# A decoder layer on one core: first transfers swapped, a root in three steps, and a last residual shared with GpSimd

## The chip, the cores and the metric

The kernel runs on one core of a Trainium2 chip. A core has five engines that run their own instruction streams and wait for one another through semaphores: TensorE (PE; its weight loads are shown as PEld), VectorE (DVE), ScalarE (ACT), GpSimd (POOL) and SyncE (SP), which here only starts transfers. Matmul results go to PSUM; everything else lies in SBUF; inputs, weights and the result lie in the chip's main memory (HBM) and come and go by DMA. The metric is the time of one execution on the device in microseconds (us), as the median of several runs.

## The reference

One decoder layer for 512 tokens of width 1024, in float32. With `rms(x, g)` for the normalisation by the root of the mean square:

```python
f = swiglu(rms_norm(h, ffn1_norm_pre[l]), ffn1_w_gate[l], ffn1_w_up[l], ffn1_w_down[l])   # width 2816
h = h + 0.5 * rms_norm(f, ffn1_norm_post[l])
u = rms_norm(h, mix_norm_pre[l])
proj = u @ w_in[l]                       # q, k, v, recurrence inputs, gates
...                                      # dilated attention and a gated linear recurrence
merged = gates[:, :, 0] * attn_d + gates[:, :, 1] * rec_d
h = h + rms_norm(merged @ w_out[l], mix_norm_post[l])
f = swiglu(rms_norm(h, ffn2_norm_pre[l]), ffn2_w_gate[l], ffn2_w_up[l], ffn2_w_down[l])
h = h + 0.5 * rms_norm(f, ffn2_norm_post[l])
```

So there are three sub-layers (feed-forward, mixer, feed-forward), each with a normalisation ahead of it and one behind it, and a residual sum.

## The kernel before

The layer is computed transposed: the 1024 channels lie on 8 chunks of 128 partitions, the 512 tokens along the free dimension. The residual stream `h` is eight chunks of 128 x 512 in two tiles of four; `hm(m, sl)` is chunk m, `hpair(m, sl)` chunks m and m + 1. Where the order matters the tokens are cut into two halves of 256 (`HALVES`).

Each float32 product is made of three matmuls (`mm3`, `seven`): weights and activations are split into a rounded high part (ScalarE copies it, L255) and the remainder (VectorE subtracts, L256), by `split`; `hi*hi`, `hi*lo` and `lo*hi` are summed in PSUM. In the feed-forwards, all but the first five of 22 inner blocks go through a scheme with seven half-size products in place of eight (`seven`, its operands made by `w_forms` and `x_forms`).

Weights are one long stream in the order of their use. SyncE's queue transfers it in groups of up to 1 MB into two buffers (`raw`, L203); a buffer is refilled when VectorE has read the group before the last. `fetch_start` does the same for the very first weights, in eight pieces of 128 x 512, interleaved with the eight token chunks: token chunk k (L238), then weight piece k (L242), with the table of gains and biases `sm` (L240) behind the first token chunk.

The start: for k = 0 to 7, `pre_norm` scales token chunk k by its gain and splits it (L342 ScalarE, L343 VectorE; the gain is in `sm`), `split` splits weight piece k, `sq_add` squares the chunk for the norm (ScalarE L314 and L317, VectorE adds, L320), and twelve matmuls follow. The root of the norm is applied behind the matmuls, since it is one factor for each token.

The root, `rstd`: a matmul with ones sums the squares over the channels (L325, L327), ScalarE takes an approximate reciprocal root `y` (L329), and VectorE refines it by one Newton step in four instructions (L330 to L333), on 256 tokens at a time. There are six such roots, twelve halves: one for each normalisation.

The end of each sub-layer, `last_product`: the last matrix product's eight chunks are added up, squared and scaled by the output gain; when the first half's sum is there, its root follows, and `residual` multiplies two chunks by the root (L357) and adds them to `h` (L358), both on VectorE. At the end of the kernel both halves take all eight chunks in this way; `to_out` sends each chunk half out on SyncE's queue as soon as it is added (L1072), 128 KB each, sixteen in all. GpSimd's queue only moves the residual stream out and in again (L673, L677, L907, L1069, L1080).

The order in which an engine's instructions stand is set by a scheduler, which takes the program text, priorities (`tc.high_priority`) and its own estimates of durations; the instruction streams are then fixed, and each engine and each queue works its stream in order, waiting where it has to. Tiles of one tag share a fixed number of buffers (`bufs`): PSUM has five of tag `acc` and three of tag `aux`, each 128 x 512.

Of the kernel before, what the change touches and what calls it, by code (L numbers as in the profile page):

```python
# [148 lines left out]
def hybrid_layer(ctx: ExitStack, tc: tile.TileContext, xT: bass.AP, wst: bass.AP, small: bass.AP,  # L149
# [23 lines left out]
    def hm(m, sl=slice(0, T)):  # L173

        return hs["t"][m // 4][:, m % 4, sl]
# [4 lines left out]
    def col(name, i):  # L180
        o, w = SMALL[name]
        return sm[:, o + i:o + i + 1]
# [50 lines left out]
    def fetch_start():  # L233

        raws = [wpool.tile([P, RAW_W], F32, name="raw", tag="raw", bufs=2) for _ in range(2)]
        wts = []
        for k in range(KC):
            nc.sync.dma_start(hm(k), xT[k])  # L238
            if k == 0:
                nc.sync.dma_start(sm, small)  # L240
            raw = raws[k // 4][:, (k % 4) * 512:(k % 4) * 512 + 512]
            nc.sync.dma_start(raw, bass.AP(tensor=wst.tensor, offset=wst.offset + k * 512 * P,  # L242
                                           ap=[[512, P], [1, 512]]))
            if k % 2 == 0:
                wt = w8()
            o = (k % 2) * 512
            wts.append((wt[:, 0, o:o + 512], wt[:, 1, o:o + 512], raw))
        state["g"], state["off"] = KC, KC * 512 * P
        return wts
# [57 lines left out]
    def ntile(name, bufs):  # L307
        return tpool.tile([P, HB], F32, name=name, tag="c", bufs=CB)
# [13 lines left out]
    def rstd(acc, r, sl, extra=None):  # L322
        for s in halves(sl):
            ps = aux_ps()[:, :HB]
            PE.matmul(ps, ones, acc[:, s], start=True, stop=extra is None)  # L325
            if extra is not None:
                PE.matmul(ps, ones, extra, start=False, stop=True)  # L327
            v, y = ntile("v", 2), ntile("y", 2)
            ACT.activation(y, ps, AF.Abs_reciprocal_sqrt, bias=eps, scale=1.0 / D)  # L329
            DVE.tensor_scalar(v, ps, 1.0 / D, EPS, op0=ALU.mult, op1=ALU.add)  # L330
            DVE.tensor_mul(v, v, y)
            DVE.scalar_tensor_tensor(v, v, -0.5, y, op0=ALU.mult, op1=ALU.mult)
            DVE.scalar_tensor_tensor(r[:, s], v, 1.5, y, op0=ALU.add, op1=ALU.mult)  # L333

    def warm(acc):
# [3 lines left out]
    def pre_norm(x, gname, m, sl):  # L339

        z = hm(m, sl)
        ACT.activation(x.hi[m][:, sl], z, AF.Copy, scale=col(gname, m))  # L342
        DVE.scalar_tensor_tensor(x.lo[m][:, sl], z, col(gname, m), x.hi[m][:, sl].bitcast(F32),  # L343
                                 op0=ALU.mult, op1=ALU.subtract)
# [5 lines left out]

    def gain(gi, m):
        return ghalf[:, gi * 8 + m:gi * 8 + m + 1] if gi is not None else col("gmb", m)

    def residual(rp, m, sl):

# [4 lines left out]
    def last_product(key, x, evac, gi, nxt, then, slots, end=False):  # L360
# [24 lines left out]
                    rstd(acc, rp, HALVES[0], tails[0])  # L385
        for sl in HALVES:
            if sl.start:
                rstd(acc, rp, sl, tails[HB])
            for m in range(KC):
                if m % 2 == 0:  # L390
                    residual(rp, m, sl)
                nxt(sl, m)
        if then:
# [250 lines left out]
    r1 = npool.tile([P, T], F32, name="r", tag="r", bufs=2)  # L644
    for k in range(KC):
        wh, wl, raw = wts[k]
        pre_norm(u1, "g1a", k, FULL)
        split(wh, wl, raw)
        sq_add(acc, lambda s: hm(k, s), FULL, k == 0)
        if k == KC - 1:  # L650
            rstd(acc, r1, FULL)
        for j in range(4):
            js = slice(j * P, (j + 1) * P)
            mm3(first[j], wh[:, js], wl[:, js], u1.hi[k], u1.lo[k], k == 0, k == KC - 1)
# [414 lines left out]
        nc.gpsimd.dma_start(kept[i], hs["t"][i].rearrange("p k t -> p (k t)"))  # L1069

    def to_out(sl, m):
        nc.sync.dma_start(out[m][:, sl], hm(m, sl))  # L1072

    def wide():
        return big([P, 2, 1024])
# [110 lines left out]
```

## Time and profile before

| | us |
|---|---|
| median of 3 runs | 1261.55 |
| lowest and highest of them | 1261.41, 1261.65 |
| the profiled execution | 1260.8 |
| its span (first to last instruction) | 1259.0 |
| TensorE busy | 1238.1 |
| VectorE busy | 970.9 |
| ScalarE busy | 705.0 |
| GpSimd busy | 20.0 |

The granted clock of TensorE is 0.997 of full speed over the span. In the rows of the timeline the columns are start, duration, engine, line, operation, output, inputs, shape and count; a bracket gives the idle time of the engine before the instruction and what ended it. Lines are those of this kernel. A matmul row's duration is longer than the step to the next one, since matmuls are pipelined: gaps are read from the brackets. "SPq" is SyncE starting a transfer. Two rows with the same start to start distance are more telling than their durations, which overlap by some hundredths where instructions of one engine follow one another.

### The profile page before, as it was taken

Reading aid. Unit: us, or ns where it says so; the run is one execution under the profiler, and the core shown is the slowest. Engines: PE = TensorE matmul, PEld = TensorE weight load, DVE = VectorE, ACT = ScalarE, POOL = GpSimd, SP = SyncE. Lnnn points to the kernel's source line nnn. Section 1 sums busy time; section 2 is a strip of 40 time slices with the busy share of each in tenths; the row PEclk is TensorE's granted clock in tenths of the full one; section 3 lists DMA queues with packets and bytes.
Section 4 is the critical chain, followed back from the end, with each engine's and each line's share of the span. In section 5 each row is a group of like instructions: output and inputs, shape, how many; then the busy total and the mean of one; then the engine's idle time right before and its main releaser. Section 6 shows DMA issues by size and latency. Waiting matters only on the chain.

```text
span 1259.0 us, 19558 instructions
## 1 busy us (share of the span) xinstructions
PE 1238.1 (98%) x7952; PEld 1127.9 (90%) x7952; DVE 970.9 (77%) x1561; ACT 705.0 (56%) x1183; POOL 20.0 (2%) x42
## 2 busy tenths in 40 slices
PE   9999999999999999999999999999999999999996
PEld 7889999999888999999988888889988999999995
DVE  7987777786588788889676987753998777777755
ACT  6555444454555565566736879436555544445543
POOL 0000000001002000000100000000000000000000
PEclk9999999999999999999999999999999999999998
DMA  6122332233514232221342231322222222223332
GB/s 240 67 92 98 106 107 106 106 108 133 202 67 157 103 107 79 74 104 68 135 144 91 87 115 67 134 99 103 101 101 92 93 100 101 101 101 117 105 130 67
DMA packets 26937, 135.66 MB, mean 108 GB/s; under 512 B 3424, under 2 KB 5600, under 8 KB 14688
## 3 DMA queue, kind: packets, MB, share of 16 engines
q1 hardware_dynamic: 24192, 122.88, 27.8%
q0 software_dynamic: 2656, 11.54, 2.7%
q8 instruction: 62, 1.02, 0.3%
q14 instruction: 27, 0.22, 0.1%
HBM read 127.07 MB, written 6.29 MB: 106 GB/s over the span
## 4 chain that ended last, share of the span: by engine, by line
PE 79%; DVE 13%; ACT 4%; DMA 2%; issue 2%; SPq 0%; DVEq 0%; ACTq 0%
PE acc L270 11%; PE acc L269 11%; PE acc L268 11%; PE acc L512 10%; PE acc L513 10%; PE acc L514 10%; DVE w L256 3%; PE aux L514 2%; PE aux L513 2%; PE aux L512 2%; DMA raw<-in_w 2%; PE acc L719 1%; ACT w L255 1%; PE acc L721 1%; PE acc L720 1%
## 5 line engine op out<-in xcount | busy, mean ns | idle before, releaser
L256 DVE TENSOR_TENSOR w<-raw,w 128x1024 fp32r<-128x1024 f32 (+2 forms) x307 | 301.7, 988 | 107.0 <-ACT w L255 106.8
L255 ACT ACTIVATE w<-raw 128x1024 fp32r<-128x1024 f32 (+2 forms) x307 | 262.3, 867 | 189.0 <-PE aux L514 55.1
L512 PE MATMUL acc<-big,w 128*128 128x256 f32 x928 | 263.4, 284 | 0.2 <-ACT c L519 0.2
L513 PE MATMUL acc<-big,w 128*128 128x256 f32 x928 | 263.4, 284 | 0.0
L514 PE MATMUL acc<-big,w 128*128 128x256 f32 x928 | 263.1, 284 | 0.0
L268 PE MATMUL acc<-act,w 128*128 128x512 f32 (+1 forms) x524 | 192.0, 367 | 2.4 <-ACT w L255 2.3
L269 PE MATMUL acc<-act,w 128*128 128x512 f32 (+1 forms) x524 | 191.5, 366 | 1.2 <-DVE act L256 1.2
L270 PE MATMUL acc<-act,w 128*128 128x512 f32 (+1 forms) x524 | 190.5, 365 | 1.6 <-DVE w L256 1.6
L512 PEld LDWEIGHTS acc<-big,w 128*128 128x128 f32 x928 | 177.8, 192 | 2.2 <-ACT c L519 0.8
L513 PEld LDWEIGHTS acc<-big,w 128*128 128x128 f32 x928 | 177.8, 192 | 1.4
L514 PEld LDWEIGHTS acc<-big,w 128*128 128x128 f32 x928 | 177.9, 192 | 0.0
L519 ACT ACTIVATE c<-acc 128x256 f32<-128x256 f32 x166 | 63.3, 382 | 97.9 <-PE acc L514 92.1
L270 PEld LDWEIGHTS acc<-act,w 128*128 128x128 f32 x524 | 98.9, 189 | 18.5 <-DVE w L256 2.9
L268 PEld LDWEIGHTS acc<-act,w 128*128 128x128 f32 x524 | 98.8, 189 | 18.5 <-ACT w L255 3.9
L269 PEld LDWEIGHTS acc<-act,w 128*128 128x128 f32 x524 | 99.0, 189 | 16.1 <-DVE act L256 1.8
L268 PE MATMUL acc<-big,w 128*128 128x512 f32 (+1 forms) x240 | 91.7, 382 | 0.0
L270 PE MATMUL acc<-big,w 128*128 128x512 f32 (+1 forms) x240 | 91.7, 382 | 0.0
L269 PE MATMUL acc<-big,w 128*128 128x512 f32 (+1 forms) x240 | 91.7, 382 | 0.0
L513 PE MATMUL aux<-big,w 128*128 128x256 f32 x272 | 77.0, 283 | 0.0
L514 PE MATMUL aux<-big,w 128*128 128x256 f32 x272 | 77.0, 283 | 0.0
L512 PE MATMUL aux<-big,w 128*128 128x256 f32 x272 | 76.9, 283 | 0.0
L256 DVE TENSOR_TENSOR w<-s,w 128x1024 fp32r<-128x1024 f32 x50 | 61.0, 1221 | 5.0 <-ACT w L255 4.9
(273 smaller groups left out, 2412.9 us busy)
## 6 DMA issues: line engine op xcount, KB each, us to landing
raw<-in_w SPq DMA_DIRECT2D x89, 1024.0 KB, 4.8
raw<-in_w SPq DMA_DIRECT2D x23, 512.0 KB, 3.6
raw<-in_w SPq DMA_DIRECT2D x6, 768.0 KB, 4.3
raw<-in_w SPq DMA_DIRECT2D x16, 256.0 KB, 3.6
raw<-in_w SPq DMA_DIRECT2D x3, 896.0 KB, 4.6
h<-in_x SPq DMA_DIRECT2D x8, 256.0 KB, 5.4
h<-in_x POOLq DMA_DIRECT2D x8, 256.0 KB, 5.2
kept_m<-h POOLq DMA_DIRECT2D x2, 1024.0 KB, 4.5
```

The source lines that it names most:

```text
L255: ACT.activation(dh, src, AF.Copy)
L256: DVE.tensor_sub(dl, src, dh.bitcast(F32))
L268: PE.matmul(ps, wh, xh, start=first, stop=False)
L269: PE.matmul(ps, wh, xl, start=False, stop=False)
L270: PE.matmul(ps, wl, xh, start=False, stop=last)
L512: PE.matmul(ps, wh, xh, start=start and k == 0, stop=False, skip_group_check=True)
L513: PE.matmul(ps, wh, xl, start=False, stop=False, skip_group_check=True)
L514: PE.matmul(ps, wl, xh, start=False, stop=k == 3, skip_group_check=True)
L519: ACT.activation(c, ps, AF.Copy)
L719: PE.matmul(pss[b], um.hi[k][:, bl], wh[:, i, :], start=k == 0, stop=False)
L720: PE.matmul(pss[b], um.hi[k][:, bl], wl[:, i, :], start=False, stop=False)
L721: PE.matmul(pss[b], um.lo[k][:, bl], wh[:, i, :], start=False, stop=k == KC - 1)
```

## The change

There are four edits.

1. In `fetch_start` the weight piece k is transferred ahead of the token chunk k, and in the loop that uses them `split` of the weights stands ahead of `pre_norm` of the tokens. The table `sm` is now third on the queue, behind the first weight piece and the first token chunk.
2. In `rstd` the step from the mean square to the root takes three VectorE instructions in place of four: `(ps + D*EPS) * y`, then times `-0.5/D * y`, then `(v + 1.5) * y`. All twelve half-roots use it.
3. For the last half of tokens at the end of the kernel a new function, `residual_end`, takes the place of four calls of `residual`. The root `rp` of that half is written to PSUM. ScalarE copies it to SBUF (`rq`); GpSimd multiplies and adds chunks 6 and 7; VectorE does chunks 0 to 5 in pairs, with its products in PSUM.
4. `to_out` sends two chunks in one transfer of 256 KB, eight transfers in place of sixteen.

```diff
         for k in range(KC):
+            raw = raws[k // 4][:, (k % 4) * 512:(k % 4) * 512 + 512]
+            nc.sync.dma_start(raw, bass.AP(tensor=wst.tensor, offset=wst.offset + k * 512 * P,
+                                           ap=[[512, P], [1, 512]]))
             nc.sync.dma_start(hm(k), xT[k])
             if k == 0:
                 nc.sync.dma_start(sm, small)
-            raw = raws[k // 4][:, (k % 4) * 512:(k % 4) * 512 + 512]
-            nc.sync.dma_start(raw, bass.AP(tensor=wst.tensor, offset=wst.offset + k * 512 * P,
-                                           ap=[[512, P], [1, 512]]))
...
             ACT.activation(y, ps, AF.Abs_reciprocal_sqrt, bias=eps, scale=1.0 / D)
-            DVE.tensor_scalar(v, ps, 1.0 / D, EPS, op0=ALU.mult, op1=ALU.add)
-            DVE.tensor_mul(v, v, y)
-            DVE.scalar_tensor_tensor(v, v, -0.5, y, op0=ALU.mult, op1=ALU.mult)
+            DVE.scalar_tensor_tensor(v, ps, D * EPS, y, op0=ALU.add, op1=ALU.mult)
+            DVE.scalar_tensor_tensor(v, v, -0.5 / D, y, op0=ALU.mult, op1=ALU.mult)
             DVE.scalar_tensor_tensor(r[:, s], v, 1.5, y, op0=ALU.add, op1=ALU.mult)
...
+    def residual_end(rp, sl):
+
+        rq = ntile("rq", 1)
+        ACT.activation(rq, rp[:, sl], AF.Copy)
+        t = tpool.tile([P, 2, HB], F32, name="res", tag="t")
+        nc.gpsimd.tensor_mul(t, facc[:, 6:8, sl], rq[:, None, :].to_broadcast([P, 2, HB]))
+        nc.gpsimd.tensor_add(hpair(6, sl), hpair(6, sl), t)
+        for m in (0, 2, 4):
+            t = acc_ps().rearrange("q (m t) -> q m t", m=2)
+            DVE.tensor_mul(t, facc[:, m:m + 2, sl], rp[:, None, sl].to_broadcast([P, 2, HB]))
+            DVE.tensor_add(hpair(m, sl), t, hpair(m, sl))
...
             if sl.start:
+                if end:
+                    rp = acc_ps()
                 rstd(acc, rp, sl, tails[HB])
+            if end and sl.start:
+                residual_end(rp, sl)
             for m in range(KC):
-                if m % 2 == 0:
+                if m % 2 == 0 and not (end and sl.start):
                     residual(rp, m, sl)
                 nxt(sl, m)
...
         wh, wl, raw = wts[k]
+        split(wh, wl, raw)
         pre_norm(u1, "g1a", k, FULL)
-        split(wh, wl, raw)
...
     def to_out(sl, m):
-        nc.sync.dma_start(out[m][:, sl], hm(m, sl))
+        if m % 2:
+            nc.sync.dma_start(out[m - 1:m + 1, :, sl].rearrange("m p t -> p m t"), hpair(m - 1, sl))
```

In the changed kernel's built instruction order three things stand that the diff doesn't show. On SyncE's queue the transfers of the last half are in the order chunks 6 and 7, then 0 and 1, 2 and 3, 4 and 5. VectorE's first product of `residual_end` waits for ScalarE's copy `rq`. On GpSimd a load of its function library stands ahead of the product, behind the last transfer of `h` and without a wait of its own.

## The prediction

> **What bounds the kernel now.** I read the page first (engine shares, chain), then TensorE's timeline for its gaps, then the chain behind each gap, and last the timelines of the start and the end, which the change touches.
>
> ```profile
> span 1259.0 us, 19558 instructions
> PE 1238.1 (98%) x7952; PEld 1127.9 (90%) x7952; DVE 970.9 (77%) x1561; ACT 705.0 (56%) x1183; POOL 20.0 (2%) x42
> PE 79%; DVE 13%; ACT 4%; DMA 2%; issue 2%; SPq 0%; DVEq 0%; ACTq 0%
> ```
>
> TensorE is busy 98% of the span and carries 79% of the chain; VectorE (DVE) carries 13%. No matmul is added or removed, so only three kinds of time can go: what lies before TensorE's first real matmul, the gaps in it, and what follows its last one. The gaps over 0.25 us between the start and the tail are few:
>
> ```profile
> 70.31 0.50 PE L270 MATMUL acc<-act,w 128*128 128x512 f32 x1 [0.74 <-DVE w L256]
> 326.30 0.50 PE L269 MATMUL acc<-act,w 128*128 128x512 f32 x1 [0.41 <-DVE act L256]
> 369.25 0.50 PE L719 MATMUL acc<-w,big 128*128 128x512 f32 x1 [0.60 <-ACT big L342]
> 911.82 0.48 PE L325 MATMUL aux<-acc,ones 128*128 128x256 f32 x1 [0.29 <-DVE acc L320]
> 955.41 0.50 PE L268 MATMUL acc<-act,w 128*128 128x512 f32 x1 [0.59 <-ACT w L255]
> 957.02 0.50 PE L270 MATMUL acc<-act,w 128*128 128x512 f32 x1 [0.88 <-DVE w L256]
> 1212.82 0.38 PE L269 MATMUL acc<-act,w 128*128 128x256 f32 x1 [0.81 <-DVE act L256]
> ```
>
> The bracket is the idle time and what ended it. Those at 70, 369 and 912 to 957 stand behind stretches in which VectorE is the late engine, and each of these stretches holds root steps (L330 to L333), which the change shortens. (Left out: three short ones inside the recurrence, which nothing here touches.) Those at 326 and 1212 have no root ahead of them; I expect them to stay.
>
> **The change, part by part.**
>
> *Root in three steps.* Each of the twelve half-roots loses one VectorE instruction.
>
> ```profile
> 28.34 0.75 DVE L331 TENSOR_TENSOR v<-v,y 128x256 f32<-128x256 f32 x2
> 29.01 0.75 DVE L332 SCALAR_TENSOR_TENSOR v<-v,y 128x256 f32<-128x256 f32 x2
> 913.52 0.42 DVE L331 TENSOR_TENSOR v<-v,y 128x256 f32<-128x256 f32 x1
> 913.98 0.43 DVE L332 SCALAR_TENSOR_TENSOR v<-v,y 128x256 f32<-128x256 f32 x1
> ```
>
> Back to back one costs half of 29.01 - 28.34, 0.335 us; where the next depends on it, 913.98 - 913.52 = 0.46. The new first step reads PSUM and y together; it runs as the other two-operand steps do, and it cannot start later than now, since the old first step also started after y.
>
> *First weights ahead of first tokens, and the split ahead of the pre-norm.*
>
> ```profile
> 0.74 0.38 SPq L238 DMA_DIRECT2D h<-in_x  x1
> 1.18 0.42 SPq L240 DMA_DIRECT2D sm<-in_small  x1
> 1.65 0.42 SPq L242 DMA_DIRECT2D raw<-in_w  x1
> 3.58 0.72 ACT L314 ACTIVATE acc<-h 128x256 f32<-128x256 f32 x2 [1.25 <-DMA h<-in_x]
> 4.21 0.70 ACT L342 ACTIVATE act<-h,sm 128x512 fp32r<-128x512 f32 x1
> 5.95 0.63 ACT L255 ACTIVATE w<-raw 128x512 fp32r<-128x512 f32 x1 [1.04 <-DMA raw<-in_w]
> 6.63 0.50 PE L268 MATMUL acc<-act,w 128*128 128x512 f32 x1 [1.46 <-ACT w L255]
> 19.23 0.75 DVE L343 SCALAR_TENSOR_TENSOR act<-h,sm,act 128x512 fp32r<-128x512 f32 x1
> 19.89 0.69 DVE L256 TENSOR_TENSOR w<-raw,w 128x512 fp32r<-128x512 f32 x1
> 20.60 4.73 DMA raw<-in_w
> ```
>
> Now the tokens land 2.84 us after their issue (0.74 to 3.58), the weights, two transfers behind, 4.30 after theirs. Swapped, weights land near 3.6 and are split while the tokens are on the way. The tokens are issued at 1.18 and land between 1.18 + 2.84 = 4.0 and 1.18 + 4.30 = 5.5; I take the middle, 4.8, because only one large transfer is ahead of them. The small gains table moves from second to third on SP's queue; the pre-norm needs it, but the two squares (0.62 us to the next start) stand first on ScalarE and cover it. Then 0.72 + 0.62 to the first matmul: about 6.15 against 6.63, 0.45 earlier (ends: 1.2 earlier, 0.2 later). From there TensorE is dense to 69.6, so this is worth something only if VectorE is earlier at 70.31 too. It is: the last first-stage split (19.89) goes ahead of the 0.66 us of L343, and it frees the buffer whose refill is the chain's transfer at 20.60; then come the first roots, 2 x 0.335. VectorE gains 0.66 + 0.67 = 1.33. At 70 TensorE can gain its gap and its earlier start, 0.74 + 0.45 = 1.19; the smaller counts: **1.2 us** (ends 0.5 and 1.35), start included.
>
> *Feed-forward to mixer, 369.* Two half-roots back to back, 0.67, against a gap of 0.60. The scheduler reorders the small VectorE instructions here, so I take **0.5** (0 to 0.6).
>
> *Mixer to second feed-forward, 880 to 957.* VectorE runs almost without pause from the second half-root there. One root step of the output norm and one of the pre-norm's first half (0.335 each) and one of its second half, alone (0.46): 1.13. TensorE's gaps are 0.29 + 0.59 + 0.88 = 1.76, so they can give it: **1.15** (0.5 to 1.76). In the built order VectorE now does two more scalings ahead of the first weight split after the root, which may open a gap near 920 that TensorE must refill from those 1.76; hence the low end.
>
> *The end.* Rows of the tail:
>
> ```profile
> 1247.78 0.47 ACT L329 ACTIVATE y<-aux,eps 128x256 f32<-128x256 f32 x1 [0.25 <-PE aux L327]
> 1248.29 0.42 DVE L330 TENSOR_SCALAR v<-aux 128x256 f32<-128x256 f32 x1 [1.75 <-ACT y L329]
> 1250.13 1.29 DVE L357 TENSOR_TENSOR res<-facc,rp 128x512 f32<-128x512 f32 x2
> 1253.74 1.29 DVE L358 TENSOR_TENSOR h<-h,res 128x512 f32<-128x512 f32 x2
> 1252.05 4.21 SPq L1072 DMA_DIRECT2D out_dram<-h  x8
> L1060 ACT ACTIVATE facc<-acc x12: 360/384/600, 848.6 to 888.9; 128x256 f32<-128x256 f32 x8, 128x512 f32<-128x512 f32 x4
> L1176 POOL MEMSET const-float32-0.0<- 128x1 f32 x1 | 0.1, 98 | 0.2 <-issue 0.2
> 26.53 1.23 DVE L256 TENSOR_TENSOR w<-raw,w 128x1024 fp32r<-128x1024 f32 x1 [3.01 <-ACT w L255]
> 1252.50:1253.00 0.50, 0.00 (x0) 0.00 (x0) 0.50 (x2) 0.00 (x0) 0.00 (x0) 0.50 0.19 63
> 1256.50:1257.00 0.50, 0.00 (x0) 0.00 (x0) 0.00 (x0) 0.00 (x0) 0.00 (x0) 0.50 0.83 270
> 1257.00:1257.50 0.50, 0.00 (x0) 0.00 (x0) 0.00 (x0) 0.00 (x0) 0.00 (x0) 0.50 0.36 119
> ```
>
> (The last three are stretches; their last two columns are the DMA engines' busy share and GB/s.) Three root steps end at 1248.29 + 3 x 0.46 = 1249.67. ScalarE's new copy of the root out of PSUM, 0.38 by L1060's 128x256 form, ends near 1250.1, and in the built order VectorE's first product waits for that copy, though it does not read it. So the product starts where it starts now: at this place the third step buys nothing. VectorE then has six instructions of 0.60 (1.20 for each two) instead of eight: done at 1253.8, not 1255.03.
>
> GpSimd has done no arithmetic in this trace. Its own rows are memsets of one column (0.10 us), no measure for 512. The bounds for one of its two instructions are VectorE's for the same shape, 0.60, and twice VectorE's for double the elements, 2 x 1.22 = 2.44. I take the middle by ratio, 1.2, which is the 26.53 row: its pair is done at 1250.1 + 2.5 = 1252.6. By the Trainium skill, GPSIMD Engine Reference, sections 3.1 and 4.1, elementwise work does not belong on GpSimd: 4497 ns against VectorE's 2293 for a two-input add of 2048 elements, my estimate 1.15 us for 512; no run here shows it yet, and the sum would be the same by it.
>
> The paired outputs of the second half stand on SP's queue in the order GpSimd's pair, then VectorE's three, so SP issues nothing before 1252.65 and three more at 0.45 each to 1254.0. One megabyte at 270 / 0.83 = 325 GB/s takes 3.2 us, first bytes some 0.8 after an issue (1252.05 to about 1252.9): the last byte at 1252.65 + 0.8 + 3.2 = 1256.65 against about 1257.2 now (119 of 270 in the last stretch, 0.2 us of it). **0.55 us** gained. With 0.60 per GpSimd instruction the last pair, ready at 1253.8, ends it, 0.8 to its first byte and 0.8 for its quarter: 1255.45, 1.75 gained. With 2.44: 1259.1, 1.9 lost.
>
> *Sum:* 1.2 + 0.5 + 1.15 + 0.55 = 3.4 us. The profiled execution took 1260.8 us beside its span of 1259.0, so 1257.4 by its own measure; the median of the runs is 0.75 above it, 1261.55, which gives 1258.15. I say 1258.1.
>
> **The rivals.**
>
> *GpSimd late.* Each instruction near 2.4 us: SP's queue holds the finished VectorE pairs behind it, the tail loses 1.9, and 2.85 - 1.9 = 0.95 is left: 1260.6. Against it, two small instructions of a plain kind; for it, an engine without one such row.
>
> *GpSimd as fast as VectorE.* Tail 1.75: 3.4 + 1.2 = 4.6, 1257.0.
>
> *The saved steps are refilled.* VectorE's earlier work meets other waits (transfers, ScalarE's order), TensorE's gaps stay, and only the end changes: 1261.55 - 0.55 = 1261.0. For it: each gap has several engines just behind it; against it: three separate stretches with VectorE on the chain.
>
> *Slower: GpSimd's code comes at its first use.* The built order puts a library load ahead of the first product, without a wait, right after the last refill of the residual:
>
> ```profile
> 1200.15 0.53 POOL L1080 DMA_DIRECT2D h<-kept  x1 [0.91 <-PE acc L514]
> 1231.04 1.28 ACT L329 ACT_TABLE_LOAD   x1
> ```
>
> From there it has 50 us to load in the shade. If the load instead falls at the product, the end moves by all of it, and from 0.55 + 2.85 = 3.4 us on the change is slower than before. ScalarE's table load, the nearest kind of row, costs 1.28 in line, too little; it takes 5.9 us to be slower by 0.2%: 1264.1. The same reference page, section 2.1, states about 6 us for the first call of a freshly loaded kernel; the time would be 1264.15, and no row here bears it out.
>
> **How the numbers follow.** Forecast 0.56, late GpSimd 0.14, fast GpSimd 0.12, refilled 0.10, load at first use 0.08. 0.2% is 2.5 us, about what a measurement of this kernel can tell from no change: the lines are 1259.0 and 1264.1. The forecast (its parts' spread gives 1257.0 to 1259.5) and the fast case are faster, nearly all; late and refilled are within; the load case is half slower, half within, and I add some for an unseen stall. Faster 0.66, same 0.27, slower 0.07. The range 1256.1 to 1260.8 holds the forecast and both GpSimd speeds and leaves out the last two cases.
>
> **What would show it.** Right: first matmul near 6.15; the gap at 70 gone or below 0.3; those at 369 and 957 smaller by what is said; those at 326 and 1212 unchanged; three root steps; VectorE's last add 1.2 us earlier; the GpSimd rows near 1.2 with SP waiting for them. Wrong: GpSimd's add ending after 1253.2 (1252.6 plus the 0.55 it has to give), tokens landing after 5.3, or a new TensorE gap at a place not listed, near 920 above all.

## The result and the profile after

The changed kernel takes 1256.75 us (median of 11 runs, 1255.09 to 1259.62) against 1261.55 of the kernel before in the same set (11 runs, 1259.63 to 1263.67): ratio 0.9964, 95% interval 0.9954 to 0.9974. That is 4.5 us faster (3.3 to 5.8), where I had forecast 1258.1. The profiled execution took 1255.59 us beside a span of 1253.8, so its span is 5.2 us shorter than before.

The page of the changed kernel, the lines that answer to those of before:

```profile
span 1253.8 us, 19539 instructions
PE 1237.8 (99%) x7952; PEld 1128.7 (90%) x7952; DVE 965.2 (77%) x1547; ACT 706.0 (56%) x1184; POOL 22.6 (2%) x44
PE 87%; DVE 8%; ACT 2%; DMA 1%; issue 1%; SPq 0%; DVEq 0%
```

TensorE does the same work in less span; VectorE's share of the chain fell from 13% to 8%. TensorE's timeline has these rows at the places that I listed before (line numbers moved by up to 16; the row at 918.45 answers to one at 920.68 in before, which my list, from 0.25 up, left out):

```profile
69.60 0.40 PE L270 MATMUL acc<-act,w 128*128 128x512 f32 x1
325.22 0.50 PE L269 MATMUL acc<-act,w 128*128 128x512 f32 x1
367.13 0.40 PE L734 MATMUL acc<-w,big 128*128 128x512 f32 x1
908.66 0.48 PE L325 MATMUL aux<-acc,ones 128*128 128x256 f32 x1 [0.27 <-DVE acc L320]
918.45 0.50 PE L270 MATMUL acc<-act,w 128*128 128x512 f32 x1 [0.34 <-DVE w L256]
953.31 0.50 PE L270 MATMUL acc<-act,w 128*128 128x512 f32 x1 [0.46 <-DVE w L256]
1208.44 0.39 PE L269 MATMUL acc<-act,w 128*128 128x256 f32 x1 [0.79 <-DVE act L256]
```

A row without a bracket did not wait long enough to be marked. The gaps at 70 and 369 are gone, of the pair at 955 and 957 one is gone and one halved, a gap of 0.34 stands near 918 where before had 0.22, and the last one is as it was. ScalarE's timeline of the start:

```profile
3.38 0.63 ACT L255 ACTIVATE w<-raw 128x512 fp32r<-128x512 f32 x1 [1.06 <-DMA raw<-in_w]
4.17 0.72 ACT L314 ACTIVATE acc<-h 128x256 f32<-128x256 f32 x2 [0.15 <-DMA h<-in_x]
4.79 0.70 ACT L341 ACTIVATE act<-h,sm 128x512 fp32r<-128x512 f32 x1
7.78 0.72 ACT L341 ACTIVATE act<-h,sm 128x512 fp32r<-128x512 f32 x1 [1.01 <-DMA h<-in_x]
```

The first tokens landed at 4.2, earlier than my 4.8, and the first real matmul came at 5.55 instead of 6.15. But the second tokens landed late, ScalarE waited 1.01 for them, and most of the early start was gone by 10 us. The tail's timeline:

```profile
1245.31 0.38 ACT L356 ACTIVATE rq<-acc 128x256 f32<-128x256 f32 x1 [1.42 <-DVE acc L332]
1245.72 1.29 DVE L362 TENSOR_TENSOR acc<-facc,acc 128x512 f32<-128x512 f32 x2 [0.45 <-ACT rq L356]
1245.77 1.26 POOL L358 TENSOR_TENSOR res<-facc,rq 128x512 f32<-128x512 f32 x1 [49.28 <-ACT rq L356]
1247.11 1.27 POOL L359 TENSOR_TENSOR h<-h,res 128x512 f32<-128x512 f32 x1
1248.84 0.69 DVE L363 TENSOR_TENSOR h<-acc,h 128x512 f32<-128x512 f32 x1
1248.41 1.98 SPq L1088 DMA_DIRECT2D out_dram<-h  x4
```

VectorE's product waits for ScalarE's copy; GpSimd takes 1.26 and 1.27; SP issues its first output 0.03 us after GpSimd's add.

To see where the 5.2 us were won, I set the start of each of the 7952 matmuls beside that of the same number in before. The difference is the lead at that point, and the table gives how much lead each stretch adds (us; times of before; the last stretch is from the last root's tail matmul, L327, to the end of the span, taken from the trace to 0.01 us). Beside the first profile of the changed kernel stand a second one of the same kernel and four of the experiments below.

| stretch | changed | again | root alone | start alone | tail alone | changed, old start |
|---|---|---|---|---|---|---|
| 0 to 27 | 0.24 | 0.83 | 0.07 | 0.41 | 0.00 | 0.04 |
| 27 to 80 | 0.58 | 0.78 | 0.72 | -0.02 | 0.12 | 0.48 |
| 80 to 340 | 0.30 | -0.42 | 0.74 | 0.71 | 0.12 | -0.11 |
| 340 to 400 | 1.15 | 1.14 | 1.18 | -0.05 | -0.08 | 1.15 |
| 400 to 967 | 1.44 | 1.40 | 1.45 | -0.07 | -0.04 | 1.45 |
| 967 to 1150 | 0.48 | 0.49 | 0.49 | 0.48 | -0.07 | 0.49 |
| 1150 to 1247 | 0.18 | -2.39 | -0.25 | -0.32 | -1.30 | -0.74 |
| 1247 to end | 0.83 | 0.82 | 0.44 | -0.01 | 0.37 | 0.82 |
| sum | 5.20 | 2.65 | 4.83 | 1.13 | -0.88 | 3.57 |

Two stretches (340 to 400 and 400 to 967) repeat to 0.05 us in the columns with the new root, and come with the root alone. The one from 1150 to 1247 differs by 2.6 us between two executions of one and the same kernel.

### The profile page after: what moved, and what is told of

It reads as the page before. It is cut to its first block, busy times and chain, and to the rows that moved or that the text cites. A ratio compares the mean times of both kernels' runs of the same rounds, so it can differ in the third digit from the quotient of the medians.

```text
span 1253.8 us, 19539 instructions
## 1 busy us (share of the span) xinstructions
PE 1237.8 (99%) x7952; PEld 1128.7 (90%) x7952; DVE 965.2 (77%) x1547; ACT 706.0 (56%) x1184; POOL 22.6 (2%) x44
## 3 DMA queue, kind: packets, MB, share of 16 engines
q0 software_dynamic: 2656, 11.54, 2.7%
## 4 chain that ended last, share of the span: by engine, by line
PE 87%; DVE 8%; ACT 2%; DMA 1%; issue 1%; SPq 0%; DVEq 0%
PE acc L269 13%; PE acc L268 13%; PE acc L270 13%; PE acc L527 11%; PE acc L528 11%; PE acc L529 11%; PE aux L529 2%; PE aux L528 2%; PE aux L527 2%; DVE w L256 2%; PE acc L736 1%; PE acc L735 1%; PE acc L734 1%; DMA raw<-in_w 1%; DVE acc L320 1%
```

## The experiments

All ratios are against runs of the kernel before on the same chip in the same set.

| kernel | median, us | ratio | 95% interval |
|---|---|---|---|
| start alone | 1260.72 | 0.9987 | 0.9978 to 0.9996 |
| root alone | 1257.84 | 0.9965 | 0.9952 to 0.9977 |
| tail alone | 1261.16 | 0.9993 | 0.9984 to 1.0002 |
| changed, GpSimd's pair on another queue | 1256.45 | 0.9957 | 0.9945 to 0.9970 |
| changed, old start | 1256.99 | 0.9958 | 0.9944 to 0.9973 |
| changed, table on ScalarE's queue | 1256.45 | 0.9949 | 0.9937 to 0.9961 |
| changed, last root in SBUF | 1256.62 | 0.9953 | 0.9941 to 0.9965 |
| changed, again | 1258.07 | 0.9958 | 0.9946 to 0.9970 |
| changed, late reload | 1254.77 | 0.9943 | 0.9931 to 0.9956 |
| changed, three edits | 1253.30 | 0.9932 | 0.9919 to 0.9944 |
| changed, without GpSimd | 1258.63 | 0.9971 | 0.9961 to 0.9981 |
| before, late reload | 1260.03 | 0.9985 | 0.9976 to 0.9993 |

### Each part alone

Start alone: the transfers swapped (weights, then tokens) and

```
+        split(wh, wl, raw)
         pre_norm(u1, "g1a", k, FULL)
-        split(wh, wl, raw)
```

> Only the start of the change, on the kernel before: each weight piece transferred ahead of its tokens, and the split issued ahead of the pre-norm; root, residual and outputs as before. Theory A (the saved 0.66 us of VectorE ahead of the first-stage split is what opens the gap at 70): the start keeps 0.24 us at 27 us, the gap of 0.74 at 70 shrinks to 0.1-0.3, TensorE is 0.7 to 0.85 us earlier at 80, and as much at the end of the span; all later gaps as before (0.41 at 326, 0.60 at 369, 0.59 and 0.88 at 956). Time 1260.8. Rival B (the gap at 70 is closed by the shorter roots, not by the start): 0.24 at 27, gap at 70 still 0.5 to 0.74, 0.2 to 0.45 earlier at the end. Time 1261.2. Rival C (whatever is won ahead of 326 is returned to the transfer that the split at 323 waits for): 0 at 327, time 1261.55.

TensorE's timeline of this kernel:

```profile
69.91 0.50 PE L270 MATMUL acc<-act,w 128*128 128x512 f32 x1 [0.31 <-DVE w L256]
368.14 0.50 PE L719 MATMUL acc<-w,big 128*128 128x512 f32 x1 [0.58 <-ACT big L342]
956.04 0.50 PE L270 MATMUL acc<-act,w 128*128 128x512 f32 x1 [0.89 <-DVE w L256]
```

The lead at 80 is 0.39, no more than at 27: that is rival B's number, though the gap at 70 shrank from 0.74 to 0.31 (A's upper edge). A gap of 0.16 at 65 is new; where the rest went I have not traced. The gaps behind the roots stayed. By the end the lead is 1.13, since the stalls at 326 and 1085 are gone, which no theory had foretold.

Root alone:

```
-            DVE.tensor_scalar(v, ps, 1.0 / D, EPS, op0=ALU.mult, op1=ALU.add)
-            DVE.tensor_mul(v, v, y)
-            DVE.scalar_tensor_tensor(v, v, -0.5, y, op0=ALU.mult, op1=ALU.mult)
+            DVE.scalar_tensor_tensor(v, ps, D * EPS, y, op0=ALU.add, op1=ALU.mult)
+            DVE.scalar_tensor_tensor(v, v, -0.5 / D, y, op0=ALU.mult, op1=ALU.mult)
```

> Only the root in three steps, on the kernel before. Theory A (each gap behind a root closes by what VectorE wins there): gap at 70 shrinks by 0.4 to 0.67, 0.9 to 1.2 us more is won by 380, 1.3 to 1.5 more by 967, and in the tail 0.46, since here nothing but the next step waits for the third one; in sum 3.0 to 4.0 us: time 1258.0. Rival B (saved steps are refilled by other waits): only the tail's 0.46 and less than 0.5 elsewhere: time 1260.9. Rival C (the gap at 70 needs both parts of the change): nothing at 70, the rest as in A: 2.6 to 3.0, time 1258.7.

TensorE's timeline:

```profile
69.49 0.50 PE L270 MATMUL acc<-act,w 128*128 128x512 f32 x1
952.87 0.50 PE L270 MATMUL acc<-act,w 128*128 128x512 f32 x1 [0.43 <-DVE w L256]
```

The span is 1254.2. Theory A holds place by place: 0.72 from 27 to 80, 1.18 from 340 to 400, 1.45 to 967, 0.44 in the tail. Its sum, 3.0 to 4.0, is passed (4.83), by the stalls at 326 and 1085, which are gone here too. Its ratio, 0.9965, is that of the whole change: by the time, the root is nearly all of it. What the rest adds does not show there; the intervals leave it up to 2 us.

Tail alone: GpSimd's pair, the copy and the paired outputs, with the root in four steps:

```
+                if end:
+                    rp = acc_ps()
                 rstd(acc, rp, sl, tails[HB])
+            if end and sl.start:
+                residual_end(rp, sl)
...
-        nc.sync.dma_start(out[m][:, sl], hm(m, sl))
+        if m % 2:
+            nc.sync.dma_start(out[m - 1:m + 1, :, sl].rearrange("m p t -> p m t"), hpair(m - 1, sl))
```

> Only the end of the change, on the kernel before: GpSimd takes chunks 6 and 7 of the second half, the root there stands in PSUM with a copy for GpSimd, outputs leave in pairs; the root still has four steps. Nothing ahead of 1247 may move. Theory A (the copy puts 0.46 us into the chain, which the third step saved in the changed kernel gives back): product 3.5 us behind the last matmul of the root (before 3.08), GpSimd's two rows 1.26 each, SP's first output 0.03 us after GpSimd's add, tail 0.3 to 0.45 us shorter than before, time 1261.2. Rival B (VectorE needn't wait for the copy where the root is longer): tail 0.8 to 0.9 shorter, time 1260.7. Rival C (pairing alone makes the tail shorter and GpSimd is beside it): tail 1.0 or more shorter.

Theory A: the tail is 0.37 shorter, and VectorE's product starts 3.50 us behind the root's tail matmul (3.08 in before, 3.04 in the changed kernel). The copy costs what the third root step saves; the time does not tell it from before. Ahead of the tail nothing of the program differs from before, and yet this profile lost 1.30 between 1150 and 1247: the unsteady stretch again.

### The end

GpSimd's pair taken off SP's queue:

```
-            nc.sync.dma_start(out[m - 1:m + 1, :, sl]...
+            q = nc.scalar if sl.start and m == 7 else nc.sync
+            q.dma_start(out[m - 1:m + 1, :, sl]...
```

> The changed kernel with one edit: GpSimd's pair of output chunks leaves by ScalarE's queue instead of standing at the head of SP's. Theory A (in the changed kernel VectorE's finished pairs wait on SP behind GpSimd's add): SP's first output of the second half starts at VectorE's first add, near 1247.6 instead of 1248.41, the outputs begin to move 0.75 us earlier, and the last byte is 0.6 to 0.8 us earlier; the last pair, ready at 1249.5, does not end it. Against before 1256.0 (the changed kernel 1256.75). Rival B (the transfers run into one another and the last pair ends them): 0 to 0.2 us won. Rival C (an issue on a second queue is slower to start and costs more than SP's): 0.2 to 0.5 us lost.

The timeline of its tail (the last root's tail matmul starts at 1246.92):

```profile
1251.36 1.27 POOL L359 TENSOR_TENSOR h<-h,res 128x512 f32<-128x512 f32 x1
1251.88 2.30 SPq L1089 DMA_DIRECT2D out_dram<-h  x3
1252.65 0.42 ACTq L1089 DMA_DIRECT2D out_dram<-h  x1
1253.09 0.69 DVE L363 TENSOR_TENSOR h<-acc,h 128x512 f32<-128x512 f32 x1
```

SP now issues 0.75 us before GpSimd is done. From the tail matmul to the end it is 10.39 us against 11.15: 0.76 won, theory A. The times can't show it (0.9957 against 0.9964, intervals overlapping). The span of this profile, 1257.3, hides it, because this execution lost 2.6 us between 1150 and 1247 (the unsteady stretch, below), and because it began badly. Its TensorE timeline at the start reads:

```profile
8.13 0.63 PE L269 MATMUL acc<-act,w 128*128 128x512 f32 x1
8.56 0.63 PE L270 MATMUL acc<-act,w 128*128 128x512 f32 x1
8.98 0.63 PE L269 MATMUL acc<-act,w 128*128 128x512 f32 x1
10.76 0.39 PE L270 MATMUL acc<-act,w 128*128 128x512 f32 x1
```

Matmuls start 0.43 us apart up to 10.3, then 0.23: TensorE ran at half speed for its first 4 us, which cost about 1.9. (The windows of the granted clock show 1.00 there, but only for want of a record: this trace's first record of the clock is at 10.31, in the other thirteen it is between 3.89 and 7.21.) By the Trainium skill, TensorE: Matmul & The Clock Gate, Part 1, the array runs at half clock until a free-running window of 3.4 us has been busy, 426.7 ns from one 512-column matmul to the next against 215.7; the 0.43 and 0.23 here agree, and that the phase differs between executions would explain why this profile has eight steps of 0.43, three others (old start, last root in SBUF, without GpSimd) one or two each, and ten none.

The last root left in SBUF for both engines, without the copy:

```
-        rq = ntile("rq", 1)
-        ACT.activation(rq, rp[:, sl], AF.Copy)
+        rq = rp[:, sl]
```

> The changed kernel with one edit: the last root of the second half stays in SBUF, both engines read it there, and ScalarE's copy for GpSimd is gone. Theory A (the copy and the wait for it stand in the chain for 0.45 us, and the third root step is used up by them): both products start 0.41 to 0.46 us earlier, 2.6 us behind the last root matmul, all else in step, the last byte and the end 0.4 to 0.5 us earlier. Rival B (VectorE and GpSimd hinder each other where both read the root in SBUF): products and adds of one or both engines grow from 0.60 and 1.26 by a tenth or more each, and 0 to 0.3 us remains, or a loss.

VectorE's rows from the view of this kernel's tile (shortest, median and longest in ns), and GpSimd's from its timeline:

```profile
L361 DVE TENSOR_TENSOR acc<-facc,rp x3: 684/699/1759, 1245.6 to 1249.1; 128x512 f32<-128x512 f32 x3
```

```profile
1245.75 1.69 POOL L357 TENSOR_TENSOR res<-facc,rp 128x512 f32<-128x512 f32 x1 [49.81 <-DVE rp L332]
1247.52 1.60 POOL L358 TENSOR_TENSOR h<-h,res 128x512 f32<-128x512 f32 x1
```

and the same view of VectorE's product in the changed kernel:

```profile
L362 DVE TENSOR_TENSOR acc<-facc,acc x3: 689/689/697, 1245.7 to 1248.1; 128x512 f32<-128x512 f32 x3
```

The products start 0.42 us earlier, as A said, but one of VectorE's products takes 1759 ns instead of 689, until GpSimd's is over, and GpSimd's take 1.69 and 1.60 instead of 1.26. The tail is 11.56 against 11.15, 0.41 longer: rival B, with a loss, by the trace; the times can't tell the two kernels apart (0.9953 against 0.9958 in the same set). So the copy is not waste; the PSUM operand that it allows keeps the two engines apart. The Trainium skill, SBUF — State Buffer, section "SBUF: two separate sides", says that a VectorE instruction with two SBUF inputs and a GpSimd instruction that reads SBUF share a pair of ports under an exclusive lock, the later one standing still for the whole of the other. These rows agree: 0.43 more on GpSimd's first product, 1.07 on VectorE's second.

VectorE doing all eight chunks, with root, start and pairing kept:

```
-                if end:
-                    rp = acc_ps()
                 rstd(acc, rp, sl, tails[HB])
-            if end and sl.start:
-                residual_end(rp, sl)
             for m in range(KC):
-                if m % 2 == 0 and not (end and sl.start):
+                if m % 2 == 0:
```

> The changed kernel with VectorE doing all eight chunks of the end again and the root in SBUF without the copy; root in three steps, start and paired outputs kept. Theory A (in the changed kernel GpSimd's pair holds up SP's queue, so its share is worth little): both are near, VectorE's product starts 0.45 us earlier and its last add ends 7.5 us behind the last root matmul instead of 6.8, but its pairs leave as they are ready; tail 10.6 to 11.1 us against 11.1, time within 0.5 us of the changed kernel's. Rival B (taking two of eight chunks off VectorE is what shortens the end): tail 11.3 to 11.6, 0.2 to 0.5 us slower.

The tail is 11.36 us against 11.15: rival B's number, but not its reason. The transfers at the end of this kernel:

```profile
1251.50:1252.00 0.50, 0.00 (x0) 0.00 (x0) 0.42 (x1) 0.00 (x0) 0.00 (x0) 0.50 0.00 0
1253.50:1254.00 0.50, 0.00 (x0) 0.00 (x0) 0.00 (x0) 0.00 (x0) 0.00 (x0) 0.50 0.59 199
```

(The last two columns are the DMA engines' busy share and GB/s.) They stand still near 1251.7, waiting for VectorE, and yet the last byte is out at 1253.90, 9.50 behind the tail matmul; in the changed kernel it is 9.84 behind, because SP waits for GpSimd. That is theory A's mechanism: in that order GpSimd's share, with the copy that it needs, makes the last byte 0.34 later. The changed kernel wins behind the last byte, where 1.30 us follow instead of 1.85. Nearly all of that is at the very end of the span, on GpSimd: from the end of the clearing of its semaphores to the end of the drain that follows, the traces show 0.56 to 0.58 us in the four profiles of kernels that give GpSimd no arithmetic, this one among them, and 0.08 or 0.09 in the ten that do. The kernel before with the late reload (below) is one of the ten, though its GpSimd only copies two columns and its outputs are single. So it is neither the number of outputs nor the work taken off VectorE; why those steps get shorter stays open.

With the pair on another queue, the last byte is 9.07 behind the tail matmul: there GpSimd's share is worth 0.43 by the last byte and 0.97 by the tail (10.39 against 11.36). The order of the queue, which the change got wrong, cost 0.76 (11.15 against 10.39). Root alone, with single outputs, has a tail of 11.54 (last byte 9.78), so pairing is worth some 0.2 to 0.3; each of these is a difference of single profiles, and three profiles with before's tail differ by 0.14 (11.85 to 11.99). The time of the kernel without GpSimd can't be told from the changed kernel's (0.9971 against 0.9964 and 0.9958, intervals overlapping).

### The start

Tokens first and pre-norm first, as before, in the changed kernel:

```
-            nc.sync.dma_start(raw, ...)
             nc.sync.dma_start(hm(k), xT[k])
             if k == 0:
                 nc.sync.dma_start(sm, small)
+            nc.sync.dma_start(raw, ...)
...
-    split(wh, wl, raw)
     pre_norm(u1, "g1a", k, FULL)
+    split(wh, wl, raw)
```

> The changed kernel without its first part: tokens ahead of weights and pre-norm ahead of split as before; root in three steps and the new end kept. Theory A (where the root is short, the start buys nothing: the root alone closed the gap at 70, and stood as far ahead at 80 as the whole change): TensorE 0.75 to 0.85 us ahead of before at 80, no gap at 70, time within 0.3 us of the changed kernel's in the same set of runs. Rival B (the parts add up, and the start is worth what it was alone): 0.4 to 1.5 us slower than the changed kernel, gap at 70 back to 0.3 or more. Rival C (the new order at the start costs something, since tokens of k=1 and the gains table come late in it): 0.3 to 0.6 us faster than the changed kernel.

Mixed. The ratio is that of the changed kernel in the same set, 0.9958 both, as theory A says, but the intervals leave room for rival B too (0.9944 to 0.9973). The trace does not agree with A: the lead at 80 is 0.52 instead of 0.75 to 0.85, and a gap of 0.23 at 70 is back. Five profiles of kernels with the new start and the new root (without a further edit to the start) stand at 0.82, 1.24, 1.47, 1.52 and 1.61 by 80, and the sixth, which began at half speed, 0.45 behind before. The two kernels with the new root and the old start stand at 0.52 and 0.79 (the 0.52 began with its first matmuls at half speed). Setting these beside each other, the start is worth 0 to 1.1 us, and kernels with the same old start and root also stand 0.7 apart there (tail alone 0.12 ahead of before, before with the late reload 0.59 behind it). So no single pair of profiles prices the start; in the time I cannot see it.

The gains table on ScalarE's queue:

```
+        nc.scalar.dma_start(sm, small)
...
-            if k == 0:
-                nc.sync.dma_start(sm, small)
```

> The changed kernel with one edit: the gains table leaves by ScalarE's queue, so that SP issues each token and weight transfer from the third on some 0.47 us earlier. Theory A (in the new order the pre-norm waits for the table, 0.57 and 0.70 us in two profiles, or the second tokens come late, 1.01 in the third): these waits of ScalarE ahead of 9 us go, TensorE stands 0.5 to 0.9 us ahead of before at 27, and the gap at 70 takes most of it back, so 0 to 0.3 us at the end. Rival B (the transfers of the start share one rate, so issuing earlier lands nothing earlier): 0.1 to 0.3 us at 27, nothing at the end. Rival C (the issue on ScalarE delays its table load and first split): later than the changed kernel by 0.1 to 0.5 us.

The lead is 1.27 at 27 and 2.32 at 80: more than A said, and what A said of the gap at 70 (that it takes most of it back) was wrong. By the time it cannot be told from the changed kernel (0.9949 against 0.9958, intervals overlapping).

### The unsteady stretch

The changed kernel once more, unaltered:

> The changed kernel once more, unaltered, to see which of the differences between the first two profiles belong to the change and which to one execution. Theory A: the gaps at 70 and 369 stay gone, that near 955 is 0.4 to 0.5, the tail behind the last root matmul is 11.1 us; what differs between executions is the start up to 10 us, the stall near 326, the one near 1085 (0.24 in one profile of before, none in the first of the changed kernel) and the wait near 1209. Time 1256.5 to 1257. Rival B: the stalls at 326 and 1085 are gone again at the same places and the same size, so that the change removed them: then they belong to the sum.

Theory A for the gap at 326 (0.87 here, none in the first profile) and for 1209, rival B for the stall at 1085, which is gone again; the time is 1 us above what I expected, but before is 1262.98 in this set, so the ratio, 0.9958, is much as it was. The granted clock by windows (the third number from the end), then the timeline:

```profile
1206.00:1208.00 2.00, 1.19 (x10) 0.99 (x9) 0.71 (x1) 1.59 (x3) 0.00 (x0) 1.00 0.10 40
1210.00:1212.00 2.00, 2.00 (x12) 2.00 (x11) 1.52 (x3) 0.42 (x1) 0.00 (x0) 0.50 0.00 0
1214.00:1216.00 2.00, 2.00 (x19) 2.00 (x18) 0.77 (x2) 0.61 (x2) 0.00 (x0) 1.00 0.00 0
```

```profile
1206.41 0.84 ACT L255 ACTIVATE big<-raw 128x768 fp32r<-128x768 f32 x1 [2.43 <-DMA raw<-in_w]
1207.83 0.51 PE L268 MATMUL acc<-act,w 128*128 128x256 f32 x2 [0.81 <-ACT act L255]
1209.50 0.38 PE L269 MATMUL acc<-act,w 128*128 128x256 f32 x1 [0.81 <-DVE act L256]
```

In the first profile ScalarE waited 1.34 for these weights, here 2.43. TensorE stood twice instead of once, and then the clock was granted at 0.50 for 3.4 us (1209.90 to 1213.31), 16 matmuls at 0.21 instead of 0.12: 1.1 and 1.5 us, the 2.6 of the table. The clock fell after 1.6 us of idling in 2.5, less than the one idle window of 3.4 us that the Trainium skill, TensorE: Matmul & The Clock Gate, Part 1, gives for it; that page's rule would not have foretold it. Nor does the length of the stalls decide it: the clock fell in the profile with GpSimd's pair on another queue too (0.97 and 0.81), but stayed at 1.00 in that without GpSimd (1.67 and 0.82) and that of the tail alone (1.20 and 0.81). What does stays open.

Beside the weights run two transfers of 1 MB that reload the residual, which is not used before 1231. So, the residual reloaded behind the last weights:

```
-    for i in range(2):
-        nc.gpsimd.dma_start(hs["t"][i]..., kept[i])
+    def reload(late):            # called where the last weights are fetched
+        for i in range(2):
+            nc.gpsimd.tensor_copy(hs["t"][i][:, 0, 0:1], late[:, 0:1].bitcast(F32))
+            nc.gpsimd.dma_start(hs["t"][i]..., kept[i])
```

> The changed kernel with one edit: the reload of the residual (two transfers of 1 MB on GpSimd's queue, issued at 1194.5 and 1196 beside the last weights) waits until the last weights have been split; GpSimd writes one element per partition of each half from that split weight ahead of its transfer, which overwrites it. First use of the residual is at 1231. Theory A (the spread between executions of one kernel comes from 1205 to 1214: the last two weight transfers share the DMA engines with the reload, land 1.3 to 2.4 us late for ScalarE, TensorE idles 0.81 to 1.6 us, and where it is the longer, the granted clock falls to 0.50 for some 3 us): without the reload beside them the weights land 1.3 us or more earlier, the gap of 0.81 near 1208 goes or falls below 0.3, no clock fall, and the executions lie within 1.5 us of each other; time 1254.5 to 1255.5, 0.8 to 2.5 us below the changed kernel's. Rival B (the weights are late because their buffer comes free late, not because of the reload): gap 0.81 as before, time as the changed kernel's. Rival C (the reload then arrives too late, or moves into the tail): slower than the changed kernel.

Theory A. Its timeline:

```profile
1204.52 0.85 ACT L255 ACTIVATE big<-raw 128x768 fp32r<-128x768 f32 x1 [0.51 <-DMA raw<-in_w]
1208.41 1.06 POOL L1102 DMA_DIRECT2D h<-kept  x2
```

ScalarE waits 0.51 instead of 1.34 or 2.43, so 0.83 or 1.9 less (A had the weights 1.3 or more earlier), there is no gap of TensorE near 1208, and the stretch 1150 to 1247 adds 1.01 us of lead (0.18 in the first profile of the changed kernel, -2.39 in the second). The last weight transfer of 384 KB lands 2.9 us after its issue; in the three profiles with a late reload it takes 2.9 to 3.1, in the eleven without 3.2 to 5.2. The five runs lie between 1254.55 and 1255.69, where the changed kernel's eleven spread over 4.5 us. By the median alone it can't be told from the changed kernel (0.9943 against 0.9958 and 0.9964, intervals overlapping).

The same edit on the kernel before:

> The kernel before with the late reload of the residual alone (GpSimd writes one element per partition from the last split weight, then reloads the residual), to price the change with the unsteady stretch at 1208 taken out of both kernels. Theory A (the stretch is as unsteady in the kernel before, and what the change is worth is what its steady places give: 0.6 to 0.9 by 80 us, 1.2 at 369, 1.45 by 958, 0.85 in the tail, 4.1 to 4.4 in all, or 4.6 to 4.9 where the stall at 1085 goes with it): gap of 0.81 near 1212 gone, executions within 2 us of each other, time 1258.9 to 1259.9, which is 4.1 to 5.0 above the changed kernel with the same edit (1254.77). Rival B (the reload matters only in the changed kernel): time and gap as before, 1261.5 or more.

Theory A in kind: the gap near 1212 is gone, and the stretch adds 0.99. The time, 1260.03, is 0.13 above its range and the spread 2.6 us instead of 2. Between the two kernels with the late reload lie 5.3 us (1260.03 to 1254.77, and as much by their ratios, since the sets differ), 0.3 above the range.

All three edits that helped by the trace (table, GpSimd's pair, reload) on the changed kernel:

> The changed kernel with three edits together: gains table on ScalarE's queue, GpSimd's output pair on ScalarE's queue, the residual reloaded behind the last weights. Theory A (they act at three places that do not touch): TensorE 2.2 to 2.4 us ahead of before at 80, tail behind the last root matmul 10.4 us (the changed kernel's 11.1), no stall of weights near 1208: span 1250.5 to 1252, time 1252.5 to 1254. Rival B (what the start wins is given back at 326, where a transfer sets the pace): 0.5 to 1 us less.

Theory A; rival B's loss at 326 is not seen (0.26 is lost near 590). Lead 2.44 at 80, tail 10.39, no stall of weights: span 1251.0, time 1253.30, ratio 0.9932 (0.9919 to 0.9944). It beats both kernels.

## Why the prediction was right, step by step

The direction and the range hold, and so does the main mechanism, the shorter root behind which TensorE's gaps close; the working of the start does not, and two terms were missing. The size was short by 1.1 us against the median of the ratio (4.5 against 3.4), and by 1.8 against the profile (5.2): 0.65 too little at 369, 0.29 at 957 and 0.28 at the end, 0.38 too much at the start, and 0.96 at places for which the sum had nothing (80 to 340, 1085, 1208).

*Start and gap at 70: 1.2 predicted, 0.82 in this profile, 1.24 to 1.61 in the others with the clock up.* The size fits the later profiles, but by luck. The first matmul came 0.6 earlier than I said, but I let it count from then on ("from there TensorE is dense"), and it did not: the second tokens were late. I also called the gains table covered by the squares; in two of the first three profiles with the new order ScalarE waited for it, 0.57 and 0.70 us. And the gap at 70 was closed by the root, not by the split: all ten profiles with the new root gain 0.48 to 1.05 from 27 to 80, the four without it -0.55 to 0.12, start alone (-0.02) among them.

*369: 0.5 predicted, 1.15 measured.* Two sizes failed. One is the ceiling: I let TensorE's gap, 0.60, bound what could be won. The rows of before's timeline around it show why it does not (the row at 369.25 stands in the prediction):

```profile
368.26 0.39 PE L721 MATMUL acc<-w,big 128*128 128x512 f32 x1
...
369.59 0.39 PE L720 MATMUL acc<-w,big 128*128 128x512 f32 x1
```

Matmuls follow each other every 0.23 us, but a row lasts 0.39, so the bracket starts counting 0.16 late; and the first one behind a stall holds the next back to 0.34. From 368.26 to 369.59 it is 1.33 where 0.46 would do: the stall cost 0.87, not 0.60. Nearly all of the other 0.28 is in late steps of the same kind: 0.18 at 362.92 and 363.25, 0.08 at 370.64.

The other is VectorE's own gain, 0.67 by my sum. Its products behind the first and the second half of this root, before and then changed:

```profile
353.53 0.69 DVE L357 TENSOR_TENSOR res<-facc,rp 128x512 f32<-128x512 f32 x1
366.76 1.29 DVE L357 TENSOR_TENSOR res<-facc,rp 128x512 f32<-128x512 f32 x2
351.96 0.68 DVE L368 TENSOR_TENSOR res<-facc,rp 128x512 f32<-128x512 f32 x1
364.43 1.29 DVE L368 TENSOR_TENSOR res<-facc,rp 128x512 f32<-128x512 f32 x2
```

The first product stands 1.57 earlier, the second 2.33; 1.12 of that was there when the stretch began, so VectorE won 1.21. The steps of the first half stand alone, and one of them is worth 0.45 there, not 0.335. Between the two products 0.76 was won, 0.33 by the second half's step and 0.33 because the built order has five square additions (L320) there and not six; the last 0.1 I have not traced.

*880 to 957: 1.15 predicted, 1.44 measured.* Here the ceiling, 1.76, did not bind; what was too small is VectorE's three steps, 1.13. Its split ahead of the matmul at 957, before and changed, and before's row near 920:

```profile
955.14 2.42 DVE L256 TENSOR_TENSOR w<-raw,w 128x1024 fp32r<-128x1024 f32 x3
951.43 2.43 DVE L256 TENSOR_TENSOR w<-raw,w 128x1024 fp32r<-128x1024 f32 x3
920.68 0.50 PE L268 MATMUL acc<-act,w 128*128 128x512 f32 x1 [0.22 <-ACT w L255]
```

The split stands 3.71 earlier, 2.27 of which was there at 400: VectorE won the 1.44. The built order of its small instructions differs here too; which of them hold the 0.31 beyond the three steps I have not traced. The gap near 920, which I had named as a sign of being wrong, grew from 0.22 to 0.34, and that is inside the 1.44.

*The end: 0.55 predicted, 0.83 and 0.82 measured.* Each step stood: GpSimd 1.26 for my 1.2, the product starting where it started, SP blocked until GpSimd is done. Two windows of the changed kernel's DMA (share and GB/s in the last columns) give the difference:

```profile
1249.50:1250.00 0.50, 0.00 (x0) 0.00 (x0) 0.04 (x1) 0.00 (x0) 0.00 (x0) 0.50 1.05 344
1252.00:1252.50 0.50, 0.00 (x0) 0.00 (x0) 0.00 (x0) 0.00 (x0) 0.00 (x0) 0.50 0.81 270
```

The last byte lies at 1252.5, 9.84 us behind the tail matmul against 10.23 before: 0.39, a little less than I said. The rest, 0.44, is behind the last byte: the span ended 1.30 us after it and 1.75 before. My sum had no term for that; it goes with GpSimd having done arithmetic, as the kernel without GpSimd shows.

*What I said would stay.* 1208 (0.79 for 0.81) did. The gap at 326 did not, 0.41 to 0.15 (too short to be marked above), but it is between 0 and 0.87 in the profiles of kernels that do not differ there: I have no reason to give it to the change. The stall of 0.24 at 1085, which I had left out as untouched, is in all three profiles of kernels with neither the new start nor the new root (0.24 to 0.30) and in none of the eleven others: 0.48 us that came with the change. In before, weights issued at 1072.85 land at 1079.3, in the start-alone kernel they take 1.4 us less. Why an earlier start or a shorter root should do that stays open.

*The rivals.* GpSimd's speed fell at the middle of my bounds, which settles late and fast GpSimd. The product began 0.08 us behind the copy's end, so no code was loaded in line (the load's two rows in the trace are at 1196.5); the 6 us of the GPSIMD Engine Reference, section 2.1 (Trainium skill) are not seen with 50 us ahead of the first use, and its sections 3.1 and 4.1, by which I estimated 1.15, agree with 1.26 on the duration. That elementwise work does not belong on GpSimd is half borne out here: in the order that the change built, it made the last byte 0.34 later, and on another queue 0.43 earlier. The refilled case is excluded by root alone.

## What to carry to other kernels

A gap of TensorE in a profile understates what the stall costs: count from start to start of the matmuls (0.87 for a bracket of 0.60 at 369, 0.48 for one of 0.24 at 1085), and the ceiling of a gain is that sum. Ask of each instruction on a queue what stands behind it: one pair at the head of SP's queue cost 0.76 us, more than the 0.21 that the work given to GpSimd won in that order. Read a gain at the end in two parts, up to the last byte and behind it, before giving it to a cause. Where executions of one kernel spread, find the stretch by setting two profiles beside each other before crediting a change with it; here a reload that nobody needed for another 25 us, moved behind the weights, was worth 0.8 us beside a good execution and 3.4 beside a bad one.

## What the runs showed of the hardware

- VectorE and GpSimd reading SBUF together, two inputs each: 1759 ns instead of 689 on VectorE and 1.69 instead of 1.26 us on GpSimd; with one operand of VectorE's in PSUM both kept their times.
- The granted clock fell to 0.50 for 3.4 us after two stalls of 0.81 within 2.5 us, and not after stalls of 1.67 and 0.82. At the start of one execution matmuls ran at half rate up to 10.3 us, where the trace's first record of the clock stands.
- Outputs of 128 KB, issued some 0.45 us apart, moved at 264 to 273 GB/s while they flowed (before); those of 256 KB moved at 332 to 354 (changed kernel).
- GpSimd's closing steps took 0.56 to 0.58 us in the four profiles of kernels without arithmetic on it and 0.08 or 0.09 in the ten with some, two copies of one column being enough.
- A weight transfer of 384 KB took 3.2 to 5.2 us beside a reload of 2 MB on GpSimd's queue, and 2.9 to 3.1 without.
